# Four more channel tiles by block products, and the fifth product ahead of the seventh

## The chip, the cores and the metric

One core of one Trainium2 chip runs the whole block. The metric is the device time of one execution in microseconds: before, the median of three runs is 1000.0 us (999.8 to 1000.95). The engines are PE (TensorE), VectorE (DVE in the profile), ScalarE (ACT), GpSimd (POOL) and SyncE (SP), whose queue issues nearly all DMAs, one after the other.

## The reference

Everything is float32; x is 1 x 1024 x 1024, D_FF is 2816. The change is in the last product and the final norm, and in how the gated product before them is handed on.

```python
y = jnp.concatenate([y_a, y_b], axis=-1)             # short gated conv, conv module
x = x + jnp.einsum("bse,ed->bsd", y, w_out[l])
h = rmsnorm(x, norm_ffn_g[l])
g = dwconv(jnp.einsum("bsd,df->bsf", h, w_gate[l]), conv_ffn_w[l])
v = jnp.einsum("bsd,df->bsf", h, w_up[l])
x = x + jnp.einsum("bsf,fd->bsd", jax.nn.silu(g) * v, w_down[l])
return rmsnorm(x, norm_final_g)
```

## The kernel before

Channels lie on the 128 partitions, tokens along the row; the 1024 tokens are two halves of 512. D_FF is 22 channel tiles, the model width 8 tiles d (KD = 8). Each float32 product is three matmuls of 128x128 weights with 128x512 data, of rounded high parts and low remainders: hi by hi, hi by lo, lo by hi. Splitting costs a rounding on ACT (`whi`, `ahi`, or `r` for data) and a subtraction on DVE (`wlo`, `alo`, `r`).

**Block products.** Two products that share their data, or two neighbouring channel tiles by two token halves, are done as a 2x2 block product with seven instead of eight block products (class `Pair`, methods m1 to m7). Data operands are B11, B21, B22 and differences T1 to T4; weight operands are A11, A12, A22 and sums S1 to S4, which POOL forms (`s`) and ACT and DVE split. PSUM bank a takes m1, then m6, m7 and m4 on top; b takes m2; c takes m5 and then m3. After each product its method `after` reads the bank as it stands then and adds it into an output; the next product on that bank has to wait for that reading. In bank a, m7 therefore waits for the reading of m6, and m4 for that of m7.

**Gate and up** run f = 0 to 21, two tiles at a time. `ff_done` makes the tile t of the gated product (convolution by ACT and DVE, silu by ACT, product by DVE). For f up to 17 POOL makes four differences of a pair of tiles, and seven stores of 256 KB put the operands into the arrays yd in DRAM. The last four tiles are stored whole into `ytail`.

**Down** takes the 18 tiles in three chunks of six. In each chunk the eight d are four pairs (d, d+1) by six tiles, PPC = 3 block columns: a product is nine matmuls. Two pairs make a couple, so there are six couples (0 and 1 of chunk 0, 2 and 3 of chunk 1, 4 and 5 of chunk 2). In a couple, `STEPS` runs each product for both pairs: m1, then m3 of the couple before, m6, m2, m7, m5, m4. Couples 1 and 3 reload each operand for the next chunk right behind the product that used it last. The residual stream is read back from `x2d` into `xd0`, `xd2`, `xd3`, `xr0` and `xr1`; the last three take the room of the tiles t (`tp.release()`), so their loads wait for what reads those tiles. For couple 0 (`early`) ACT copies the bank a (`a1`) and POOL adds the copy; elsewhere DVE adds from the bank.

**The tail** multiplies the last four tiles plainly: for each of two halves and eight d, 4 tiles x 3 = 12 matmuls (`tail_mm`), 192 in all, the first half through before the second. The first half's final norm (sum of squares, a matmul with ones, root, reciprocal, products on POOL) lies beside the second half's matmuls. The second half's last output is done in three pieces of columns, with products on DVE (d < 5) and POOL.

PE follows the written order with few exceptions, and in the last part so do DVE, ACT and POOL. On the other queues the order comes from the scheduler, with work marked `urgent` first.

Of the kernel before, what the change touches and what calls it, by code (L numbers as in the profile page):

```python
# [13 lines left out]
P = 128  # L14
# [12 lines left out]
NTAIL = NF - 2 * NCH * PPC  # L27
# [18 lines left out]
def block_kernel(ctx: ExitStack, tc, xT, win01, win, wout, wgate, wup, wdown, consts, outT):  # L46
# [364 lines left out]
    yd = {o: dpool.tile([P, NCH * PPC, H], F32, name=f"yd{o}") for o in OPS}  # L411
    ytail = dpool.tile([NTAIL, P, S], F32, name="ytail")

# [90 lines left out]
    class Sums:  # L504
# [12 lines left out]
        def first(self, g, v):  # L517
# [4 lines left out]
            s1, s2 = self.both(hilo())  # L522
            return {"S1": s1, "S2": s2}
# [83 lines left out]
    def ff_done(f, g, v):  # L607
# [7 lines left out]
        if f >= NF - NTAIL:  # L615
            nc.sync.dma_start(ytail[f - (NF - NTAIL)], cc)
            return
# [110 lines left out]
    def ff_prep(f):  # L728
        raw, hl = g_job(f)
# [11 lines left out]
    with tc.manual_schedule(engines={nc.tensor.engine, V.engine}):  # L741
# [45 lines left out]
        p2.w.update(s2.second(g2[0], up2))  # L787
        plain[1].second_b()
# [5 lines left out]
    with tc.manual_schedule(engines={nc.tensor.engine}):  # L794
        for p in plain:
            p.finish()
        for f in range(NHEAD, NF - 2):
            p, q = fp[f], fp[f + 1]
            ff_prep(f + 1)
# [12 lines left out]

    W3 = PPC * P
    rblocks = [R[i][:, j, :] for i in (2, 3, 0, 1, 4, 5) for j in range(8)]

    def xblock(o, k, z):
        return rblocks[OPS.index(o) * 2 * PPC + z * PPC + k]
# [5 lines left out]
    def load_op(ch, o):  # L823
        for k in range(PPC):
            load_split(xblock(o, k, 0), xblock(o, k, 1), yd[o][:, ch * PPC + k, :])

    def load_d(p, tag, d, ch):
        t = p.tile([P, 2 * W3], F32, tag=tag, name=tag)
        f0 = 2 * PPC * ch
        for e in range(2):  # L830
            nc.sync.dma_start(
                t[:, e * W3 : e * W3 + W3].rearrange("p (f m) -> p f m", m=P),
                wdown[d, :, f0 : f0 + 2 * PPC].rearrange("p (f e) m -> p e f m", e=2)[:, e])
        return t

    w34 = [R[5][:, 2 + 3 * e : 5 + 3 * e, :].rearrange("p b t -> p (b t)") for e in range(2)]

    class Down(Pair):
        def __init__(self, ch, dp):
            super().__init__(PPC, lambda o, k: (xblock(o, k, 0), xblock(o, k, 1)))  # L840
            self.ch, self.dp, self.e = ch, dp, dp % 2
            self.early = ch == 0 and dp < 2

        def prep1(self):
            self.raw = load_d(wraw, "raw", 2 * self.dp, self.ch)
            hl = [t[:, : 2 * W3] for t in hilo()]
            split(self.raw, *hl, nc.vector)
            self.w.update(g_parts(hl, PPC))

        def prep2(self):  # L850
            self.up = load_d((rup, rup2)[self.e], "up", 2 * self.dp + 1, self.ch)
            self.s = Sums(PPC)
            self.w.update(self.s.first(self.raw, self.up))

        def prep3(self):
            t = w34[self.e]
            self.w.update(self.s.second(self.raw, self.up, a22p, (t[:, : 2 * W3], t[:, 2 * W3 :])))

# [39 lines left out]
    couples = [[Down(ch, 2 * i + e) for e in range(2)] for ch in range(NCH) for i in range(2)]  # L898

# [9 lines left out]
    STEPS = (("m6", "T2"), ("m2", "B21"), ("m7", "T3"), ("m5", "T1"), ("m4", "T4"))  # L909
# [37 lines left out]
    with tc.manual_schedule(engines={nc.tensor.engine}):  # L947
        for d in range(3, KD):
            load_xd(d)
        for i, pair in enumerate(couples):  # L950
            ch = pair[0].ch
            reload = i % 2 and ch + 1 < NCH
# [13 lines left out]
            for step, o in STEPS:  # L966
                for p in pair:
                    getattr(p, step)()
                if reload:
                    load_op(ch + 1, o)  # L970


    free = rblocks[:16]

    def yblock(h, i, z):
        return free[h * 8 + 2 * i + z]

    def load_tail(h):
        for i in range(NTAIL):
            load_split(yblock(h, i, 0), yblock(h, i, 1), ytail[i, :, h * H : h * H + H])  # L980

    tw = {}

    def tail_prep(dp):
        hl = hilo()
        for e in range(2):
            d = 2 * dp + e
            raw = wraw.tile([P, NTAIL * P], F32, tag="raw", name="rawt")
            nc.sync.dma_start(raw.rearrange("p (f m) -> p f m", m=P), wdown[d, :, NF - NTAIL :])
            a = e * NTAIL * P  # L990
            sl = [t[:, a : a + NTAIL * P] for t in hl]
            split(raw, *sl, nc.vector)
            tw[d] = parts(sl, 0, NTAIL)

    def tail_mm(b, d, h):
        for i in range(NTAIL):
            mm3(b, tw[d][0][:, i, :], tw[d][1][:, i, :], yblock(h, i, 0), yblock(h, i, 1), i == 0, i == NTAIL - 1)

    load_tail(0)
    tail_prep(0)  # L1000
    b0 = []
    with tc.manual_schedule(engines={nc.tensor.engine}):
        for d in range(2):
            b0.append(bank("y"))
            tail_mm(b0[d], d, 0)
        for p in couples[-1]:
            p.m3()
    load_tail(1)
    rf = rup.tile([P, S], F32, tag="up", name="rf")

    def scr(name):
        return cpy.tile([P, H], F32, tag="c", name=name)

    acc3 = wsum.tile([P, S], F32, tag="s", name="acc")
    accs = [half(acc3, h) for h in range(2)]
# [10 lines left out]
    def done(b, d, h):  # L1026
        x = half(xf[d], h)
        nc.vector.tensor_tensor(out=x, in0=b, in1=x, op=ALU.add)
        sq = scr("sq") if d else accs[h]
        nc.scalar.activation(sq, x, AF.Square)  # L1030
        if d and (h, d) != (1, KD - 2):
            nc.vector.tensor_tensor(out=accs[h], in0=accs[h], in1=sq, op=ALU.add)
# [14 lines left out]

    with tc.manual_schedule(engines={nc.tensor.engine}):
        for d in range(KD):
            if d >= 2:  # L1050
                if d % 2 == 0:
                    tail_prep(d // 2)
                b0.append(bank("y"))
                tail_mm(b0[d], d, 0)
            done(b0[d], d, 0)
            scale(d, 0)
    with tc.manual_schedule(engines={e.engine for e in (nc.tensor, nc.vector, nc.scalar, nc.gpsimd)}):
        for d in range(KD - 1):
            b = bank("y")
            tail_mm(b, d, 1)  # L1060
            if d == 1:
                m0 = total3(accs[0])
            s6 = done(b, d, 1)
            scale(d, 1)
            if d == 1:
                std = scr("std")
                nc.scalar.activation(std, m0, AF.Sqrt, bias=eps_r, scale=1.0 / D)
            if d == 2:
                nc.vector.reciprocal(rf[:, :H], std)
                for dd in range(KD):  # L1070
                    fin(dd, 0, 0, H, nc.gpsimd)
                    if dd % 2:
                        store(dd // 2, 0, 0, H)
        last = bank("y")
        tail_mm(last, KD - 1, 1)
        x = half(xf[KD - 1], 1)
# [10 lines left out]
        for (a, b), m in zip(PIECES, ms):  # L1087
            nc.scalar.activation(std[:, a:b], m[:, a:b], AF.Sqrt, bias=eps_r, scale=1.0 / D)
            if a == 0:
                scale(KD - 1, 1)  # L1090
# [7 lines left out]
    for p in (xlp, rup2, cpy, rup, wsum, xrp, a22p, psm, ps, dpool, wspl, wraw, apool, cpool):  # L1098
# [52 lines left out]
```

## Time and profile before

| | |
|---|---|
| median of three runs | 1000.0 us |
| profiled execution | 1000.93 us |
| its span | 999.1 us |
| instructions | 11602 |
| mean granted TensorE clock | 0.993 |
| matmul records on PE | 4208 |
| DMA, read and written | 84.79 and 27.00 MB |

Times in rows are microseconds from the span's start. A row of a timeline gives start, length, engine, line, operation, output and inputs, and how many instructions were drawn together; the bracket has the idle time before it and what ended it. Gate and up end near 760, couples 0 to 5 run from there to 933.8, the tail to 982, and what follows is the end of the norm. PE overlaps neighbouring matmuls, so the spacing of starts, not the length of one, tells its pace.

### The profile page before, as it was taken

What the parts mean: (1) busy time and instruction counts of PE and PEld (TensorE: products, weight loads), DVE (VectorE), ACT (ScalarE), POOL (GpSimd) and SP (SyncE); (2) the same over time, 40 slices, a digit from 0 to 9 for tenths busy, and PEclk for the clock granted to TensorE, in tenths of its full rate; (3) what the DMA queues carried; (4) which work ended last, traced back from release to release, by engine and by line L of the source; (5) the groups of instructions that cost most, each with busy time, mean ns of one, the idle gap of its engine ahead of it and who ended that gap; (6) DMA issues with size and microseconds to landing.
All of it is one profiled execution on the core that took longest, in us unless ns stands there. A gap on an engine that the chain in (4) does not pass through costs nothing.

```text
span 999.1 us, 11602 instructions
## 1 busy us (share of the span) xinstructions
PE 967.5 (97%) x4208; PEld 790.8 (79%) x4208; DVE 755.6 (76%) x888; ACT 452.8 (45%) x632; POOL 477.0 (48%) x303
## 2 busy tenths in 40 slices
PE   7999999999999999999999999999998999999994
PEld 5788888888878887788888888888886787878883
DVE  7899999999578897855655565565569798796556
ACT  7454422234564456434444443444457263544353
POOL 4289754353853006554455456365336744352006
PEclk9999999999999999999999999999999999999998
DMA  6211111113554204143143133134284663643105
GB/s 257 85 44 63 43 45 61 42 64 106 193 190 153 76 0 158 64 148 106 64 145 108 64 124 129 64 101 141 70 287 130 220 207 96 194 127 109 61 1 169
DMA packets 63274, 112.56 MB, mean 113 GB/s; under 512 B 5488, under 2 KB 27120, under 8 KB 62960
## 3 DMA queue, kind: packets, MB, share of 16 engines
q1 hardware_dynamic: 62640, 110.65, 33.1%
q10 hardware_dynamic: 576, 1.17, 0.3%
q8 instruction: 33, 0.54, 0.2%
q14 instruction: 25, 0.20, 0.1%
HBM read 84.79 MB, written 27.00 MB: 112 GB/s over the span
## 4 chain that ended last, share of the span: by engine, by line
PE 81%; DVE 9%; ACT 3%; issue 2%; DMA 1%; POOL 1%; POOLq 0%; SPq 0%; DVEq 0%; ACTq 0%
PE a L557 30%; PE mm L166 20%; PE c L557 15%; PE b L557 7%; DVE r L93 2%; PE c L692 1%; PE a L692 1%; PE mm L153 1%; PE mm L152 1%; PE mm L154 1%; PE y L154 1%; PE y L152 1%; PE y L153 1%; DMA raw<-wgate 1%; ACT whi L131 1%
## 5 line engine op out<-in xcount | busy, mean ns | idle before, releaser
L166 PE MATMUL mm<-r,whi 128*128 128x512 f32 x576 | 155.8, 389 | 0.0
L557 PE MATMUL a<-r,whi 128*128 128x512 f32 x472 | 145.7, 390 | 0.4 <-ACT a L542 0.4
L323 DVE SCALAR_TENSOR_TENSOR cv<-u,cst,cv 128x512 f32<-128x512 f32 x203 | 138.9, 751 | 1.7 <-ACT cv L317 1.2
L511 POOL TENSOR_TENSOR s<-raw,s 128x512 f32<-128x512 f32 (+1 forms) x31 | 57.5, 1854 | 161.5 <-DVE wlo L93 161.5
L166 PEld LDWEIGHTS mm<-r,whi 128*128 128x128 f32 x576 | 108.1, 188 | 22.6
L557 PE MATMUL c<-r,whi 128*128 128x512 f32 x392 | 121.1, 390 | 0.0
L93 POOL TENSOR_TENSOR wlo<-raw,whi 128x1024 fp32r<-128x1024 f32 x30 | 77.5, 2586 | 88.0 <-ACT whi L131 88.0
L131 ACT ACTIVATE whi<-raw 128x1024 fp32r<-128x1024 f32 (+1 forms) x68 | 69.2, 1020 | 103.5 <-PE mm L166 32.0
L557 PEld LDWEIGHTS a<-r,whi 128*128 128x128 f32 x472 | 88.4, 188 | 19.7 <-ACT a L542 0.8
L511 POOL TENSOR_TENSOR s<-up 128x512 f32<-128x512 f32 (+1 forms) x31 | 42.0, 1354 | 116.7 <-DMA up<-wup 96.8
L557 PE MATMUL a<-r,wlo 128*128 128x512 f32 x236 | 92.2, 391 | 2.8 <-DVE wlo L93 2.8
L166 PE MATMUL mm<-r,wlo 128*128 128x512 f32 x288 | 90.0, 389 | 0.0
L557 PEld LDWEIGHTS c<-r,whi 128*128 128x128 f32 x392 | 73.8, 188 | 16.0
L542 ACT ACTIVATE a<-a 128x512 f32<-128x512 f32 x80 | 47.5, 595 | 66.9 <-PE a L557 64.2
L131 ACT ACTIVATE whi<-s 128x1024 fp32r<-128x1024 f32 (+1 forms) x52 | 52.5, 1010 | 53.5 <-PE c L557 39.8
L557 PE MATMUL c<-r,wlo 128*128 128x512 f32 x196 | 76.5, 390 | 0.0
L635 DVE TENSOR_TENSOR t<-a,c 128x512 f32<-128x512 f32 x40 | 27.5, 687 | 64.4 <-ACT a L542 38.1
L557 PE MATMUL a<-r,ahi 128*128 128x512 f32 x224 | 70.5, 396 | 1.4 <-ACT a L542 1.4
L557 PE MATMUL b<-r,whi 128*128 128x512 f32 x232 | 71.4, 389 | 0.0
L93 DVE TENSOR_TENSOR wlo<-s,whi 128x1024 fp32r<-128x1024 f32 (+1 forms) x52 | 64.2, 1236 | 5.8 <-ACT whi L131 5.7
L131 ACT ACTIVATE r<-r 128x512 fp32r<-128x512 f32 x71 | 43.8, 628 | 49.8 <-DMA r<-ydB 23.3
L166 PEld LDWEIGHTS mm<-r,wlo 128*128 128x128 f32 x288 | 54.1, 188 | 11.2
(214 smaller groups left out, 2142.0 us busy)
## 6 DMA issues: line engine op xcount, KB each, us to landing
raw<-wgate SPq DMA_DIRECT2D x22, 512.0 KB, 4.9
up<-wup SPq DMA_DIRECT2D x20, 512.0 KB, 3.6
raw<-win SPq DMA_DIRECT2D x18, 512.0 KB, 3.2
ydT<-t SPq DMA_DIRECT2D x36, 256.0 KB, 3.4
r<-ydT SPq DMA_DIRECT2D x36, 256.0 KB, 3.3
raw<-wout SPq DMA_DIRECT2D x16, 512.0 KB, 3.4
ydB<-t SPq DMA_DIRECT2D x27, 256.0 KB, 5.0
r<-ydB SPq DMA_DIRECT2D x27, 256.0 KB, 4.5
```

The source lines that it names most:

```text
L93: eng.tensor_tensor(out=out, in0=a, in1=b, op=ALU.subtract)
L131: nc.scalar.activation(hi, y, AF.Copy)
L152: nc.tensor.matmul(out, whi, hi, start=first, stop=False)
L153: nc.tensor.matmul(out, whi, lo, start=False, stop=False)
L154: nc.tensor.matmul(out, wlo, hi, start=False, stop=last)
L166: nc.tensor.matmul(outs[h], w, a[h][z], start=s0, stop=s1)
L323: nc.vector.scalar_tensor_tensor(fin if k == KC - 1 else acc, src, w, acc, ALU.mult, ALU.add)
L511: self.eng.tensor_tensor(out=self.t[:, i * self.w : (i + 1) * self.w], in0=a, in1=b, op=op)
L542: nc.scalar.activation(t, b, AF.Copy)
L557: nc.tensor.matmul(out, w[wz][:, k, :], x[xz], start=first and k + wz + xz == 0, stop=k == n - 1 and wz == 1, skip_group_check=not first)
L635: nc.vector.tensor_tensor(out=out, in0=a, in1=b, op=op)
L692: nc.tensor.matmul(out, w[wz][:, k, :], xz, start=first and k == 0 and wz == 0 and xz is hi, stop=not first and k == 3 and wz == 1)
```

## The change

- `NTAIL` and `ytail` are gone. The last four channel tiles are a fourth chunk (`NPL` = 2 block columns, products of six matmuls) of four pairs `fin4` = a4, b4, c4, d4: 28 products, 168 matmuls. The tiles f = 18 to 21 thus get POOL's differences and seven stores per pair in place of one store of 512 KB per tile.
- For all four pairs the products that give the first token half (m1, m6, m2, m7, m4) come ahead of m5 and m3, which give the second.
- `STEPS` has m5 ahead of m7 in all couples, and T1 and T3 are both loaded behind m7. Couples 1, 3 and now 5 reload.
- Squares of the second half are partly added on POOL; in the three pieces DVE does 8, 6 and 5 of the eight products, not 5, 5 and 5.
- A gate weight load (`job`) is written ahead of `plain[1].second_b()`; no row of any engine stands elsewhere for it.

```diff
-NTAIL = NF - 2 * NCH * PPC
+NPL = NF // 2 - NCH * PPC
...
-        if f >= NF - NTAIL:
-            nc.sync.dma_start(ytail[f - (NF - NTAIL)], cc)
-            return
         ys[f] = cc
...
+    fin4 = [Down(NCH, dp) for dp in range(2)]
+    fin4 += [Down(NCH, 2 + e, rblocks[28 + 2 * e : 30 + 2 * e], rblocks[32 + 2 * e : 34 + 2 * e]) for e in range(2)]
+    couples.append(fin4[:2])
...
-    STEPS = (("m6", "T2"), ("m2", "B21"), ("m7", "T3"), ("m5", "T1"), ("m4", "T4"))
+    STEPS = (("m6", ("T2",)), ("m2", ("B21",)), ("m5", ()), ("m7", ("T3", "T1")), ("m4", ("T4",)))
...
-            reload = i % 2 and ch + 1 < NCH
+            reload = i % 2
...
+    def final(d, h, eng=nc.vector, first=0, alone=None):
         x = half(xf[d], h)
+        sq = scr("sq") if d != first else accs[h]
         nc.scalar.activation(sq, x, AF.Square)
+        if d not in (first, alone):
+            eng.tensor_tensor(out=accs[h], in0=accs[h], in1=sq, op=ALU.add)
+        scale(d, h)
         return sq
...
+        for p in (a4, b4):
+            p.m6()
...
+        for p in (a4, b4):
+            p.m2()
+            final(2 * p.dp, 0)
...
+        for p in (c4, d4):
+            p.m4()
+            final(2 * p.dp + 1, 0)
...
+        a4.m5()
+        b4.m5()
+        m0 = total3(accs[0])
+        final(1, 1, first=1)
+        std = scr("std")
+        nc.scalar.activation(std, m0, AF.Sqrt, bias=eps_r, scale=1.0 / D)
+        final(3, 1, nc.gpsimd, 1)
+        c4.m5()
+        nc.vector.reciprocal(rf[:, :H], std)
+        d4.m5()
+        final(5, 1, nc.gpsimd, 1)
+        final(7, 1, nc.gpsimd, 1)
+        for dd in range(KD):
+            fin(dd, 0, 0, H, nc.gpsimd)
...
+        a4.m3()
+        final(0, 1, first=1)
+        b4.m3()
+        final(2, 1, first=1)
+        c4.m3()
+        s6 = final(4, 1, first=1, alone=4)
+        d4.mul(d4.c, "S4", "B22", False)
...
-        for (a, b), m in zip(PIECES, ms):
+        for (a, b), m, n in zip(PIECES, ms, (KD, 6, 5)):
...
-                fin(d, 1, a, b, *((nc.vector, rp) if d < 5 else (nc.gpsimd,)))
+                fin(d, 1, a, b, *((nc.vector, rp) if d < n else (nc.gpsimd,)))
```

Three places show how instructions move. A row gives line, operation, output and inputs with the tile's size, and how many follow one another. Line numbers of the changed kernel are a few lower or higher.

The first is SP's queue of DMAs at the end of gate and up, while couple 0 runs. Before:

```order
L616 DMA ytail<-t 128x1024 x2
L907 DMA xd_5699<-x2d 128x1024
L907 DMA xr_5700<-x2d 128x1024 x2
L907 DMA xr_5701<-x2d 128x1024 x2
L831 DMA raw<-wdown 128x3x128 x2
```

And with the change, the names ydB and ydT standing for B11, T1, B21, B22 and then T2, T3, T4:

```order
L623 DMA ydB_1797<-t 128x512
L831 DMA raw<-wdown 128x3x128 x2
L623 DMA ydT_1792<-t 128x512
L831 DMA up<-wdown 128x3x128 x2
L623 DMA ydT_1794<-t 128x512
L831 DMA raw<-wdown 128x3x128 x2
L819 DMA r_96<-ydB_1791 128x512
L623 DMA ydT_1796<-t 128x512
L819 DMA r_96<-ydB_1791 128x512 x2
L831 DMA up<-wdown 128x3x128 x2
L912 DMA xd_5720<-x2d 128x1024
L912 DMA xr_5721<-x2d 128x1024 x2
```

The loads of xd3 (`xd_5699`, then `xd_5720`) and xr0 stood right behind the two stores; now the seven stores of the last pair, all loads of the next couple's weights and three of r stand ahead of them.

The second is ACT at the same time: `a_5840` and `a_5852` before, `a_5883` and `a_5895` after, are the copies of bank a behind m7 of couple 0; `whi<-s` rounds the sums S1, S2 of couple 1, and `t` is the last silu. Before:

```order
L131 ACTIVATE r_99<-s 128x768
L131 ACTIVATE whi<-raw 128x768 x2
L542 ACTIVATE a_5840<-a 128x512
L613 ACTIVATE t<-t 128x1024
L542 ACTIVATE a_5852<-a 128x512
L131 ACTIVATE whi<-s 128x768 x2
```

After:

```order
L131 ACTIVATE r_99<-s 128x768
L131 ACTIVATE whi<-raw 128x768 x2
L131 ACTIVATE whi<-s 128x768
L612 ACTIVATE t<-t 128x1024
L131 ACTIVATE whi<-s 128x768
L541 ACTIVATE a_5883<-a 128x512
L541 ACTIVATE a_5895<-a 128x512
```

Both copies are now behind both roundings of sums.

The third is DVE in couple 1, which is also how couple 3 reads; `xr` with input a is the reading of bank a, the first of each pair behind m7, that with c is behind m5. Before:

```order
L93 TENSOR_TENSOR r_94<-r_94,r_97 128x512
L863 TENSOR_TENSOR xr_5700<-xr_5700,a 128x512
L93 TENSOR_TENSOR r_94<-r_94,r_97 128x512
L863 TENSOR_TENSOR xr_5701<-xr_5701,a 128x512
L93 TENSOR_TENSOR r_94<-r_94 128x512 x2
L863 TENSOR_TENSOR xr_5700<-xr_5700,c 128x512
```

After:

```order
L93 TENSOR_TENSOR r_94<-r_94,r_97 128x512
L865 TENSOR_TENSOR xr_5721<-xr_5721,c 128x512
L93 TENSOR_TENSOR wlo<-s,whi 128x768
L93 TENSOR_TENSOR r_94<-r_94,r_97 128x512
L865 TENSOR_TENSOR xr_5722<-xr_5722,c 128x512
L93 TENSOR_TENSOR wlo<-s,whi 128x768
L93 TENSOR_TENSOR r_95<-r_95 128x512 x2
L865 TENSOR_TENSOR xr_5721<-xr_5721,a 128x512
```

The reading behind m7 now follows the two readings behind m5, two splits of sums, a split of B21 and two splits of T1 for the next chunk, and m4 of the first pair comes directly behind the second pair's m7 on PE.

More of the change, by code (lines that the diff above doesn't have):

```diff
@@ L949, in block_kernel @@
             load_xd(d)
-        for i, pair in enumerate(couples):
+        for i, pair in enumerate(couples[:-1]):
             ch = pair[0].ch
-            reload = i % 2 and ch + 1 < NCH
+            reload = i % 2
             for p in pair:
@@ L969, in block_kernel @@
                 if reload:
[L970 to L1009, printed above, removed]
+                    for o in ops:
+                        load_op(ch + 1, o)
+    tq = open_pool("tq", 1)
+    accs = [tq.tile([P, H], F32, name=f"acc3{h}") for h in range(2)]
+    rf = None
     def scr(name):
         return cpy.tile([P, H], F32, tag="c", name=name)
-    acc3 = wsum.tile([P, S], F32, tag="s", name="acc")
-    accs = [half(acc3, h) for h in range(2)]
     def total3(a):
@@ L1046, in store @@
         nc.sync.dma_start(outT[2 * dp : 2 * dp + 2, :, cols].rearrange("k p t -> p k t"), src)
+    a4, b4, c4, d4 = fin4
     with tc.manual_schedule(engines={nc.tensor.engine}):
[L1049 to L1056, printed above, removed]
-    with tc.manual_schedule(engines={e.engine for e in (nc.tensor, nc.vector, nc.scalar, nc.gpsimd)}):
[L1058 to L1076, printed above, removed]
```

94 lines of the change are left out of this document (62 added, 32 removed).

## The prediction

> **What bounds the kernel now.** I read the page's busy shares first, then the table of stretches, then the timelines of single engines where the changed code runs. In the table a row gives the stretch, its length, then busy time and count for PE, weight loads, DVE (VectorE), ACT (ScalarE) and POOL, then the granted clock, DMA share and GB/s.
>
> ```profile
> PE 967.5 (97%) x4208; PEld 790.8 (79%) x4208; DVE 755.6 (76%) x888; ACT 452.8 (45%) x632; POOL 477.0 (48%) x303
> ...
> 760.00:780.00 20.00, 15.50 (x58) 11.47 (x57) 20.00 (x15) 10.85 (x16) 19.02 (x11) 0.91 0.35 106
> ...
> 860.00:880.00 20.00, 20.00 (x89) 16.46 (x88) 20.00 (x27) 11.32 (x18) 9.62 (x7) 1.00 0.56 174
> 880.00:900.00 20.00, 19.56 (x87) 15.88 (x86) 17.76 (x23) 8.78 (x13) 8.37 (x6) 1.00 0.43 128
> ...
> 980.00:999.00 19.00, 5.76 (x29) 4.41 (x28) 12.84 (x26) 5.20 (x11) 10.61 (x14) 0.80 0.57 188
> ```
>
> PE sets the end: in the full stretch 860 to 880 it starts 89 matmuls, more closely one every 0.227 us (below: 796.08 - 787.89 = 8.19 for the 36 of four products). Nine (a product of three pairs) take 2.04 us and six 1.36. In the part that the change touches it loses time only at the seventh products of couples 0, 2 and 4 (rows below) and after 982. DVE is full or nearly so where this happens, and POOL with it in the first stretch. Whatever is put ahead of a DVE or POOL result there is paid by PE. Times below are those of the profiled execution (1000.93 us, span 999.1); the median is 0.9 less.
>
> **Couple 0: fifth ahead of seventh product.** Timeline rows: start, length, engine, line, output and inputs, and in brackets the idle time and its releaser.
>
> ```profile
> 769.98 0.61 PE L557 MATMUL a<-r,r 128*128 128x512 f32 x2
> 771.23 2.33 PE L557 MATMUL a<-r,r 128*128 128x512 f32 x9 [0.64 <-DVE r L93]
> ...
> 776.33 3.35 PE L557 MATMUL a<-r,r 128*128 128x512 f32 x7 [2.76 <-DVE r L93]
> 779.48 0.71 PE L557 MATMUL c<-r,whi 128*128 128x512 f32 x2
> ...
> 787.89 0.62 PE L557 MATMUL a<-r,whi 128*128 128x512 f32 x2
> ...
> 796.08 0.61 PE L557 MATMUL a<-r,whi 128*128 128x512 f32 x2
> ```
>
> Before, the two m7 wait 0.64 and 2.76 us for VectorE's splits of S3, and the seven matmuls behind the second wait take 3.15 us instead of 1.6: a clock loss of 1.5. With both m5 first (4.1 us from 769.98), m7 starts at 774.1 and ends at 778.2; both waits go. What is late next is m4(0). It adds to m7's bank, so it needs ACT's copy of m7, and in the order above that copy now stands behind two roundings of sums and a silu; the second sum comes from POOL.
>
> ```profile
> 774.26 2.01 DVE L93 TENSOR_TENSOR r<-s,r 128x768 fp32r<-128x768 f32 x1
> 781.52 2.32 DVE L614 TENSOR_TENSOR t<-t 128x1024 f32<-128x1024 f32 x1
> 789.37 0.69 DVE L863 TENSOR_TENSOR xd<-xd,a 128x512 f32<-128x512 f32 x1 [1.91 <-DMA xd<-x2d]
> ...
> 777.10 1.99 POOL L511 TENSOR_TENSOR s<-up 128x384 f32<-128x384 f32 x1
> 779.17 1.61 POOL L511 TENSOR_TENSOR s<-s,raw 128x384 f32<-128x384 f32 x1
> 788.30 1.01 POOL L511 TENSOR_TENSOR s<-raw,s 128x384 f32<-128x384 f32 x1
> 791.83 1.28 POOL L90 TENSOR_TENSOR xr<-xr,a 128x512 f32<-128x512 f32 x1
> ...
> 781.67 0.85 ACT L131 ACTIVATE whi<-s 128x768 fp32r<-128x768 f32 x1 [1.35 <-PE c L557]
> 790.16 0.60 ACT L542 ACTIVATE a<-a 128x512 f32<-128x512 f32 x1 [1.77 <-PE a L557]
> ...
> 774.36 9.84 SPq L616 DMA_DIRECT2D ytail<-t  x2
> 784.30 0.38 SPq L907 DMA_DIRECT2D xd<-x2d  x1
> 795.59 1.50 SPq L820 DMA_DIRECT2D r<-ydB  x3
> ...
> xr<-x2d SPq DMA_DIRECT2D x4, 512.0 KB, 6.3
> ytail<-t SPq DMA_DIRECT2D x1, 512.0 KB, 3.0
> ```
>
> POOL's first sum is done when its next operation starts, at 777.1; then a new difference t<-t (1.3 to 2.0, taken 1.7), 1.99, 1.61: 782.5. ACT: rounding 0.85, copy 0.60: 784.1. PE waits 5.9 us, and I charge the same clock loss of 1.5: m4 ends at 789.7 against 787.89. With POOL at its short rows (1.0 and 1.28) the copy comes at 781.9 and nothing is lost.
>
> Then m1 of couple 1 and m3(0) run to 795.8, and **m3(1) is late**. Its bank must first be read by VectorE into xd3, and xd3's load moved: before it was issued 0.1 us behind the second ytail store, now it stands behind seven stores for the tail pair, in one in-order queue. The last, ydT4, needs POOL's last difference. VectorE's product t, 2.32 long, moves behind two more instructions to 785.5 (the addition of c, 0.6, and a split, 0.95); POOL then does an addition, two t, two s and the last t: six operations of 1.01 to 1.6, about 1.3 each, from 785.9 to 793.8. Behind ydT4 the queue issues two loads of r (0.5 each) and two of up, and xd3 goes out at 796.3. Before, VectorE used it 5.1 us after issue (784.30 to 789.37), waiting on it; with 4.7 it is there at 801. Addition 0.7, m3(1) 2.04, a second clock loss 1.5: couple 1's m6 starts at 805.3, not 796.08. **Term: +9.2.** Bounds: POOL at its short rows and a load of 3.0 (the DMA view's landing of the ytail store) give +4.7; POOL at 1.6 and a load of 6.3 (that of the four xr loads) give +12.4.
>
> On the clock loss, the Trainium skill (TensorE: Matmul & The Clock Gate, What's actually happening) puts the drop to half speed behind an idle window of about 3.4 us, and as long again of work to undo it; the wait of 2.76 above already shows it. By its figures the two long waits lose some 1.7 each, an estimate, and the term would be +9.6.
>
> **Couples 1 and 3.** Here T1 and T3 are both loaded behind m7, and m4(0) needs VectorE's addition of m7.
>
> ```profile
> 810.89 0.67 DVE L863 TENSOR_TENSOR xr<-xr,a 128x512 f32<-128x512 f32 x1
> 813.89 0.68 DVE L863 TENSOR_TENSOR xr<-xr,c 128x512 f32<-128x512 f32 x1
> 814.49 0.95 DVE L93 TENSOR_TENSOR wlo<-s,whi 128x768 fp32r<-128x768 f32 x1
> 815.36 0.68 DVE L93 TENSOR_TENSOR r<-r 128x512 fp32r<-128x512 f32 x1
> 817.66 2.93 DVE L93 TENSOR_TENSOR r<-r 128x512 fp32r<-128x512 f32 x2
> 868.97 0.68 DVE L863 TENSOR_TENSOR xr<-xr,a 128x512 f32<-128x512 f32 x1
> ...
> 812.40 0.63 PE L557 MATMUL a<-r,ahi 128*128 128x512 f32 x2
> 871.49 0.63 PE L557 MATMUL a<-r,ahi 128*128 128x512 f32 x2
> 834.52 3.67 PE L557 MATMUL a<-r,r 128*128 128x512 f32 x15 [1.41 <-DVE xd L863]
> 892.64 3.66 PE L557 MATMUL a<-r,r 128*128 128x512 f32 x15 [0.44 <-DVE xd L863]
> ```
>
> Seven instructions newly stand ahead of that addition: two of c and three of r at 0.6 (813.89 to 814.49), two wlo<-s at 0.87: 4.8 us. In an engine as full as before the addition ends at 810.89 + 4.8 + 0.6 = 816.3, and m4(0), due at 812.40, waits 3.9; in couple 3, 868.97 + 5.4 = 874.4 against 871.49: 2.9. If PE's long waits let VectorE catch up, the wait falls towards nothing, but POOL's sums of this couple run beside it (two splits took 2.93 there, not 1.36). Between 0 and 3.9, and 0 and 2.9, I take 2.6 and 2.0, two thirds, as the row with POOL beside it is the nearer one. The waits of couples 2 and 4 (1.41, 0.44) go, since m5's 4.1 us cover them. **Term: +4.6 - 1.8 = +2.8**, bounds -1.8 and +5.0. Couple 5 also reloads, but ten matmuls of the next chunk and of m3 lie between m7 and m4: nothing, as long as VectorE is within 2.3 us.
>
> The Trainium skill (SBUF — State Buffer, Who interferes with whom) has VectorE and POOL exclude each other for a whole instruction when VectorE reads two SBUF operands. The pair at 2.93 agrees, while additions from PSUM keep 0.68; by it a split could wait out a POOL operation of up to 2.0, and the term would reach its upper bound.
>
> **The tail.** 192 plain matmuls become 168: 24 x 0.227 = -5.4 for PE. But the last matmul isn't the end.
>
> ```profile
> 970.91 3.35 DVE L1069 RECIPROCAL rf<-std 128x512 f32<-128x512 f32 x1
> 977.55 1.66 DVE L1032 TENSOR_TENSOR acc<-acc,sq 128x512 f32<-128x512 f32 x1 [0.70 <-ACT sq L1030]
> 982.68 0.34 DVE L1080 TENSOR_TENSOR xr<-y,xr 128x192 f32<-128x192 f32 x1
> ...
> 974.40 5.95 POOL L1037 TENSOR_TENSOR xd<-xd,rf 128x512 f32<-128x512 f32 x4 [63.03 <-DVE rf L1069]
> ...
> 987.79 1.15 DVE L1037 TENSOR_TENSOR xd<-xd,rp 128x192 f32<-128x192 f32 x4 [0.40 <-ACT rf L1093]
> ```
>
> Before, matmuls of the second half lay beside the norm of the first. Now the first half's last m4 ends at 933.80 (start of the tail) + 150 x 0.227 = 967.8, nothing covers its sum, and 36 matmuls follow (8.2 us). From 967.8 one chain leads to the first piece: addition 0.6, square 0.65, sum 0.7, matmul 0.9, root 0.7, wait for an addition 0.9, reciprocal 3.35, addition 0.6, square 0.65, POOL's new sum 1.3, sum 0.7, addition 0.6, square 0.65, sum beside POOL's products 1.65, addition 0.6: 14.6, with some 0.05 per hand-over 15.3. First piece at 983.1, against 982.68. PE itself is done at 979. So the 5.4 are eaten by VectorE, and four more products at 0.29 (1.15/4) in the pieces add 1.2. **Term: +1.6**, bounds -4.2 (all 5.4 kept) and +3.
>
> **At nothing:** `job` moves no instruction. The pair 18/19 gets four POOL operations and 0.75 MB more of stores in 735 to 757; PE's matmuls there are ten us and more from the loads behind them, without which cover it is 0.7.
>
> **Sum:** +9.2 + 2.8 + 1.6 = +13.6: 1014.5 against 1000.93, 1013.6 against the median.
>
> **Rivals.** (1) Couple 0 costs only its lower bound and VectorE has caught up by couple 3: +4.7 + 0.5 + 1.6 = +6.8, 1006.8. For it: POOL's rows of 1.0 at 788; against: VectorE is 100% busy until 785, and POOL's rows beside that are 1.6 to 2.2. (2) **Not slower:** VectorE and POOL hardly meet, because PE's waits spread their work. Every split then takes 0.69, every POOL sum 1.0, the product t 1.2: xd3 goes out at 793.3, lands in 3.0, m6 starts at 799.1 (+3.0); couples 1 and 3 don't wait (-1.8); the tail follows PE (-3.2 + 1.2 = -2.0): -0.8, 999.2. It decides if POOL's rows behind 777 have a mean under 1.1. Against it: the rows at 777 and 779. (3) The upper bounds of couples 0 and 1 meet: +12.4 + 5.0 + 1.6 = +19, 1019.
>
> **How the numbers follow.** Forecast (1008 to 1018) 0.57, rival 1 (1001 to 1008) 0.2, rival 2 (under 1001) 0.15, rival 3 0.08. A measurement tells 0.2% from no change: under 998 is 0.1 (half of rival 2 and what beats it), within 998 to 1002 is 0.07, above is 0.83. The range runs from 1000 to 1018.5, leaving out 0.11 below and 0.08 above.
>
> **What would show it.** Right: no wait at m7 of couples 0, 2, 4; at m4(0) of couple 0 a wait of 4 to 6 us for ACT's copy; at m3(1) one of 4 to 7 for VectorE, which waits for the load of xd3, issued after 794; 1 to 4 us at m4 of couples 1 and 3; some 2 us at the total in the tail; the first piece 3 us or more behind the last product. Wrong, if xd3 is issued before 789 or VectorE's first piece follows the last matmul at once.

## The result, and the profile after

The changed kernel is slower, by two and a half times what was forecast: 1033.22 us median (1030.51 to 1035.42) against 999.9 us, a ratio of 1.0331 with an interval of 1.030 to 1.0361. The profiled execution took 1035.42 us, its span is 1033.3 us against 999.1, so the trace has 34.2 us to explain. One execution of the kernel with both copies, below, took 1590.72 us at a granted clock of 0.571 and is left out of its median.

Here are the first part of the page after, and rows of its table of stretches with the same columns as before. The stretch 1000 to 1033 answers to 980 to 999 of before.

```profile
PE 976.4 (95%) x4184; PEld 796.6 (77%) x4184; DVE 771.0 (75%) x911; ACT 461.6 (45%) x650; POOL 507.4 (49%) x330
...
780.00:800.00 20.00, 12.11 (x45) 9.53 (x45) 11.27 (x10) 5.06 (x8) 15.41 (x11) 0.83 0.49 158
...
860.00:880.00 20.00, 20.00 (x89) 16.46 (x88) 10.32 (x15) 6.32 (x11) 8.73 (x8) 1.00 0.51 152
880.00:900.00 20.00, 16.20 (x62) 12.84 (x61) 17.28 (x25) 10.35 (x17) 5.87 (x4) 0.83 0.55 164
...
960.00:980.00 20.00, 16.82 (x62) 13.05 (x61) 16.59 (x24) 9.31 (x18) 8.70 (x10) 0.83 0.11 31
...
1000.00:1033.00 33.00, 16.53 (x56) 12.96 (x56) 21.31 (x37) 12.64 (x22) 17.29 (x16) 0.72 0.38 127
```

The count behind PE is what to read: 89 matmuls fill 20 us, and three of these stretches start only 45 to 62. In each of those three the granted clock is below 1 as well, so PE loses twice, by waiting and by running slowly afterwards. The stretch 860 to 880 is as full as before: where PE doesn't wait, its pace is the same.

The view of waits names what PE waits for between 735 and 1030. A row gives the waiting engine, its output and line, whom it waits for, then the sum, the times and the longest, in us.

```profile
PE c L556 <- DVE xd L865: 8.7, 1, 8.7
PE a L556 <- DVE xr L865: 7.4, 2, 3.8
PE a L556 <- ACT a L541: 6.8, 3, 5.8
PE total L1086 <- DVE acc L1000: 4.6, 1, 4.6
PE a L556 <- DVE xd L865: 2.3, 1, 2.3
PE total L988 <- DVE acc L1000: 2.2, 1, 2.2
```

All but the totals are waits for a PSUM bank that has not been read yet: c at m3(1) in couple 1, a at m4 of couples 1 and 3 (7.4 in two), a at m4(0) of couple 0 (5.8 of the 6.8), and a once more in the tail. The number in brackets is the pair: m4(0) is m4 of a couple's first pair, and m3(1) is m3 of couple 0's second pair, which runs within couple 1.

The last row of products in the timeline of PE, and the first of the pieces in VectorE's:

```profile
1000.76 10.32 PE L556 MATMUL c<-r,r 128*128 128x512 f32 x36
```

```profile
1016.11 0.34 DVE L1083 TENSOR_TENSOR xr<-c,xr 128x192 f32<-128x192 f32 x1
```

PE is done with them at 1011.1, 5.0 us ahead of the first piece, where before the first piece followed at once.

Starts of the same product in both timelines of PE cut the 34.2 us into the prediction's terms:

| from, to | before | after | grown by | predicted |
|---|---|---|---|---|
| start, behind m2 of couple 0 | 769.98 | 771.57 | 1.6 | 0 |
| to m6 of couple 1 | 796.08 | 810.11 | 12.4 | 9.2 |
| to m6 of couple 5 | 913.28 | 936.65 | 9.3 | 2.8 |
| to the end of the last product | 982.5 | 1011.1 | 5.2 | -3.2 |
| to the end of the span | 999.1 | 1033.3 | 5.6 | 4.8 |

### The profile page after: what moved, and what is told of

Its sections match the earlier page's. It is cut to its first block, busy times and chain, and to the rows that moved or that the text cites. A ratio compares the mean times of both kernels' runs of the same rounds, so it can differ in the third digit from the quotient of the medians.

```text
span 1033.3 us, 11698 instructions
## 1 busy us (share of the span) xinstructions
PE 976.4 (95%) x4184; PEld 796.6 (77%) x4184; DVE 771.0 (75%) x911; ACT 461.6 (45%) x650; POOL 507.4 (49%) x330
## 3 DMA queue, kind: packets, MB, share of 16 engines
q1 hardware_dynamic: 68144, 113.79, 33.3%
## 4 chain that ended last, share of the span: by engine, by line
PE 73%; DVE 10%; issue 5%; DMA 5%; POOL 3%; ACT 3%; SPq 0%; POOLq 0%; DVEq 0%; ACTq 0%
PE a L556 28%; PE mm L166 19%; PE c L556 13%; PE b L556 6%; DVE r L93 3%; POOL s L510 2%; PE c L688 1%; PE a L688 1%; DMA xd<-x2d 1%; PE mm L154 1%; PE mm L153 1%; PE mm L152 1%; DVE wlo L93 1%; DMA c<-xT 1%; DMA raw<-wgate 1%
## 5 line engine op out<-in xcount | busy, mean ns | idle before, releaser
L556 PE MATMUL a<-r,whi 128*128 128x512 f32 x496 | 155.5, 395 | 0.2 <-ACT a L541 0.2
L510 POOL TENSOR_TENSOR s<-raw,s 128x512 f32<-128x512 f32 (+2 forms) x35 | 61.8, 1767 | 162.3 <-DVE wlo L93 153.8
L131 ACT ACTIVATE whi<-raw 128x1024 fp32r<-128x1024 f32 (+2 forms) x72 | 71.7, 998 | 108.5 <-PE b L556 36.9
L556 PEld LDWEIGHTS a<-r,whi 128*128 128x128 f32 x496 | 94.5, 191 | 21.0 <-ACT a L541 0.6
L510 POOL TENSOR_TENSOR s<-up 128x512 f32<-128x512 f32 (+2 forms) x35 | 45.8, 1310 | 119.5 <-DMA up<-wup 97.6
L556 PE MATMUL a<-r,wlo 128*128 128x512 f32 x248 | 97.9, 395 | 2.9 <-DVE wlo L93 2.9
L556 PE MATMUL a<-r,ahi 128*128 128x512 f32 x240 | 80.1, 416 | 14.5 <-DVE xr L865 7.4
L90 POOL TENSOR_TENSOR t<-t 128x512 f32<-128x512 f32 x44 | 67.7, 1550 | 20.1 <-DVE t L613 20.1
L131 ACT ACTIVATE whi<-s 128x1024 fp32r<-128x1024 f32 (+2 forms) x54 | 53.8, 996 | 47.4 <-PE c L556 33.9
L93 DVE TENSOR_TENSOR wlo<-s,whi 128x1024 fp32r<-128x1024 f32 (+2 forms) x54 | 66.6, 1234 | 5.8 <-ACT whi L131 5.7
```

What stands on the lines that cost most here:

```text
L90: nc.gpsimd.tensor_tensor(out=out, in0=a, in1=b, op=op)
L93: eng.tensor_tensor(out=out, in0=a, in1=b, op=ALU.subtract)
L131: nc.scalar.activation(hi, y, AF.Copy)
L510: self.eng.tensor_tensor(out=self.t[:, i * self.w : (i + 1) * self.w], in0=a, in1=b, op=op)
L556: nc.tensor.matmul(out, w[wz][:, k, :], x[xz], start=first and k + wz + xz == 0, stop=k == n - 1 and wz == 1, skip_group_check=not first)
```

## The experiments

The theory after the result: the new order moves the reading of the bank that frees PE behind other work in an in-order queue, on VectorE in couples 1 and 3, on ScalarE in couple 0, and on SP (the load of xd3) ahead of m3(1). The rivals: the engines have too much work wherever the banks are read, or the four channel tiles cost the time whatever the order. Each ratio is against the kernel before on the same chip.

| kernel | median us | before | ratio, 95% interval |
|---|---|---|---|
| after | 1033.22 | 999.9 | 1.0331 (1.030 to 1.0361) |
| after, old order of products | 1010.17 | 1000.36 | 1.0096 (1.0081 to 1.0111) |
| before, new order of products | 1016.35 | 1000.36 | 1.0154 (1.0139 to 1.017) |
| that, bank a copied in couples 1, 3 | 1005.57 | 1000.25 | 1.0062 (1.0046 to 1.0078) |
| after, bank c copied in couple 0 | 1028.01 | 1000.36 | 1.0275 (1.0259 to 1.029) |
| after, both copies | 1019.49 | 1000.49 | 1.0193 (1.0173 to 1.0213) |
| before, with the added stores | 1006.66 | 1000.49 | 1.0059 (1.0044 to 1.0074) |
| after, other weight tiles in the tail | 1029.89 | 1000.36 | 1.0291 (1.0274 to 1.0308) |
| after, reciprocal earlier | 1029.97 | 1000.25 | 1.0304 (1.029 to 1.0318) |
| after, old order, all mends together | 1009.96 | 1000.25 | 1.0096 (1.0081 to 1.011) |
| before, new order in couples 2, 4 | 999.74 | 1000.25 | 0.9996 (0.9987 to 1.0005) |
| that, bank a copied there | 998.44 | 1000.57 | 0.9982 (0.9973 to 0.9991) |

### The two halves of the change apart

After, with the old order of products:

```diff
-    STEPS = (("m6", ("T2",)), ("m2", ("B21",)), ("m5", ()), ("m7", ("T3", "T1")), ("m4", ("T4",)))
+    STEPS = (("m6", ("T2",)), ("m2", ("B21",)), ("m7", ("T3",)), ("m5", ("T1",)), ("m4", ("T4",)))
```

> The changed kernel with the old order of products (seventh ahead of fifth, T3 loaded behind the seventh and T1 behind the fifth); the fourth chunk by products stays. Theory (the order of the products makes the waits at m4): the waits at m4 of couples 0, 1 and 3 with the slow clock behind them (about 7.8, 5.6 and 6.6 us) go, the old ones at m7 of couples 0, 2 and 4 come back (about 7 in all), the wait of m3 for xd3's load stays at some 8 us: about 1020 us. Rival (the added work of the fourth chunk loads VectorE and POOL, and the order of products matters little): within 4 us of 1033.

Before, with the new order, is the same line the other way round.

> The kernel before with the new order of products alone (fifth ahead of seventh, T1 and T3 both loaded behind the seventh); the last four tiles stay plain. Theory: m4 waits some 4 us in couple 0 and 4 each in couples 1 and 3, with 1.5 to 2.5 of slow clock behind each, the old waits at m7 (about 7 us) go, xd3's load is in time: +8 to +11, about 1010 us. Rival (the order is harmless without the stores): within 2 us of 1000.

The order is worth 23 us in the kernel after (1033.2 to 1010.2), and 16 us alone. The four tiles alone cost 9.8 us; 16.0 and 9.8 leave 7.5 of the 33.3 us to the two together. Both theories named the right side and missed the size: the old order gains 10 us more than expected, the new order alone costs 5 to 8 us more. Waits of PE from 760 on with the old order after:

```profile
PE a L556 <- DVE r L93: 3.4, 2, 2.8
PE c L556 <- DVE xd L865: 3.3, 1, 3.3
```

The waits at m7 are those of before (3.4 in two). That for xd at m3(1) is 3.3, and was expected to stay near 8: the four tiles bring it, and the new order makes it 8.7. With the new order alone, couples 1 and 3 are worse than in the kernel after, not better; the timelines of PE and then of VectorE in couple 1 of that kernel:

```profile
807.87 4.24 PE L557 MATMUL a<-r,r 128*128 128x512 f32 x18
820.64 1.22 PE L557 MATMUL a<-r,ahi 128*128 128x512 f32 x2 [8.53 <-DVE xr L863]
```

```profile
803.84 1.41 DVE L93 TENSOR_TENSOR r<-r 128x512 fp32r<-128x512 f32 x2 [4.56 <-ACT r L131]
...
813.37 0.68 DVE L863 TENSOR_TENSOR xr<-xr,c 128x512 f32<-128x512 f32 x1
813.97 0.94 DVE L93 TENSOR_TENSOR wlo<-s,whi 128x768 fp32r<-128x768 f32 x1
814.84 0.68 DVE L93 TENSOR_TENSOR r<-r,r 128x512 fp32r<-128x512 f32 x1
815.44 0.68 DVE L863 TENSOR_TENSOR xr<-xr,c 128x512 f32<-128x512 f32 x1
816.04 1.15 DVE L93 TENSOR_TENSOR wlo<-s,whi 128x768 fp32r<-128x768 f32 x1
817.11 2.88 DVE L93 TENSOR_TENSOR r<-r 128x512 fp32r<-128x512 f32 x2
819.91 0.67 DVE L863 TENSOR_TENSOR xr<-xr,a 128x512 f32<-128x512 f32 x1
```

PE is done with both m7 at 812.1 (807.87 + 4.24), and the first pair's bank a is read at 819.91. From 803.84 on VectorE works without a gap, in the end at the seven instructions that the prediction had counted. It starts late, since its reload splits had waited 4.56 us for ScalarE's roundings, and ScalarE 6.65 us for the reload's DMA. The first row is ScalarE's, the second VectorE's split at the same place in the kernel before, 2.5 us earlier:

```profile
803.18 1.35 ACT L131 ACTIVATE r<-r 128x512 fp32r<-128x512 f32 x2 [6.65 <-DMA r<-ydB]
```

```profile
801.30 2.52 DVE L93 TENSOR_TENSOR r<-r 128x512 fp32r<-128x512 f32 x2 [2.29 <-ACT r L131]
```

And the seven take 6.5 us (813.37 to 819.91), not 4.8: the two splits at 817.11 take 2.88 beside GpSimd's sums, where the prediction had counted 0.6 for each.

So 8.5 us are lost in couple 1 (and 2.7 more to the clock), where the bound of the prediction was 3.9.

### Is it the queue or the work?

The same kernel, with bank a behind m7 copied out by ScalarE in couples 1 and 3 and added by GpSimd, as couple 0 does:

```diff
-            if self.early:
+            if self.early or (m, self.ch < 2, self.dp >= 2) == (1, True, True):
                 self.add_copy(m, h, copy_of(self.a, "a1"))
```

> The kernel before with the new order of products alone (as the run of that alone, 1016.4 us), where in couples 1 and 3 ACT copies bank a behind m7 and POOL adds the copy, so that m4 needn't wait for VectorE's queue. Theory (m4 waits because the reading stands behind some 16 us of work in VectorE's in-order queue): the waits of 8.7 and 4.3 us at m4 fall to 0 to 3 each, and the slow clock behind them goes too: 1002 to 1007 us. Rival (m4 waits for the loads of T1, whoever reads the bank, since ACT's copies also stand behind their rounding): 1012 us or longer.

Four readings leave VectorE, and 10.8 of the 16.0 us come back (1016.35 to 1005.57). The wait in couple 1 falls to 0.9 and that in couple 3 to 0.3; 2.8 us of waiting turn up at m4 of couple 2 instead. What cost the time was mostly the queue in which the reading stood, and not how much there was to do: the four readings themselves are 2.7 us of VectorE's work, at 0.68 each.

### m3(1), and why mends don't add up

After, with bank c of couple 0 copied by ScalarE, so that m3(1) no longer waits for xd3:

```diff
-            self.add(1, 1, self.c)
+            if self.early:
+                self.add_copy(1, 1, copy_of(self.c, "c1"))
+            else:
+                self.add(1, 1, self.c)
```

> The changed kernel, where in couple 0 ACT copies bank c behind m5 and POOL adds the copy (as is done there for bank a), so that m3 doesn't wait for xd3's load. Theory: the wait of 8.9 us at m3 of couple 0 goes, with 1.6 of slow clock: -8 to -10.5, about 1023 to 1025 us, with m4 of couple 1 waiting as before. Rival (the engines are behind there anyway, and the next product waits instead): less than 4 us are won.

Its waits for a bank between 760 and 1030:

```profile
PE a L556 <- DVE xr L865: 14.9, 2, 10.8
PE a L556 <- ACT a L541: 5.8, 1, 5.8
```

The wait of 8.7 is gone, but only 5 us come back, of the 8 to 10.5 expected: at m4 of couple 1 the wait rose from 3.6 to 10.8. While PE stood at m3(1), VectorE had caught up. The wait at m3(1) had hidden most of the wait behind it, which is why couple 1 looked milder in the kernel after than with the order alone. Then both copies at once, the last two diffs on the kernel after:

> The kernel after, with bank c of couple 0 and bank a behind m7 of couples 1 and 3 copied out by ScalarE, so that VectorE's queue stands ahead of no bank that m3(1) or m4 of couples 1 and 3 waits for. Theory (the order of the products costs what it does because PE waits for VectorE's in-order queue, and each copy alone only uncovered the next wait): with all of them gone at once the couples lose their waits, m3(1) under 2 us, m4 of couples 1 and 3 under 1 us each, with the clock losses behind them; 1012 to 1016 us. Rival (the work of VectorE and ScalarE is what PE runs into, wherever the banks are read): the waits move on to m7 of the even couples or to the weights' tiles; 1022 us or longer.

It lies between the two: 13.7 us come back, of the 17 to 21 of the theory. m3(1) no longer waits, and m4 of couple 3 waits 0.1 us; m4 of couple 2 now waits 1.9. In couple 1 the reading has changed engines and is late again. PE and ScalarE there:

```profile
814.68 1.29 PE L556 MATMUL a<-r,r 128*128 128x512 f32 x5
820.53 1.22 PE L556 MATMUL a<-r,ahi 128*128 128x512 f32 x2 [4.55 <-ACT a L541]
```

```profile
813.45 1.96 ACT L131 ACTIVATE r<-r 128x512 fp32r<-128x512 f32 x3 [4.97 <-DMA r<-ydT]
...
818.34 1.66 ACT L131 ACTIVATE r<-r 128x512 fp32r<-128x512 f32 x3
819.90 1.06 ACT L541 ACTIVATE a<-a 128x512 f32<-128x512 f32 x2
```

ScalarE had 5 us of nothing to do, waiting for a reload's DMA, and then ran eleven roundings of operands and sums ahead of the copy. The queue explains it here too; my theory had the wait gone because the copy was on another engine, and that step was wrong.

### What the stores alone cost

Before, with the differences and seven stores per pair for the last four tiles added (what they store is not used):

```diff
-    yd = {o: dpool.tile([P, NCH * PPC, H], F32, name=f"yd{o}") for o in OPS}
+    yd = {o: dpool.tile([P, NF // 2, H], F32, name=f"yd{o}") for o in OPS}
...
             nc.sync.dma_start(ytail[f - (NF - NTAIL)], cc)
-            return
```

> The kernel before, with GpSimd's differences and the seven stores of the first half's rows for the last four channel tiles added beside the stores of the old tail; what they store is not used, and the tail is the old one. Theory (about a third of what the four tiles cost comes ahead of the tail, from these stores: 0.6 us at the end of the feed-forward part and the wait of m3(1) for the late xd3): a wait of 2 to 4 us at the first product that reads xd3 in couple 1, and about 1004 us. Rival (the stores cost nothing there, all that the four tiles cost comes from the tail): no such wait, within 1 us of the kernel before.

It costs 6.2 us, more than expected, with no change of order and with the old tail. SP's queue, and PE at m3(1):

```profile
783.45 1.24 SPq L626 DMA_DIRECT2D ydB<-t  x2
785.93 3.85 SPq L626 DMA_DIRECT2D ydT<-t  x3
791.72 0.38 SPq L830 DMA_DIRECT2D raw<-wdown  x1
792.19 0.44 SPq L906 DMA_DIRECT2D xd<-x2d  x1
```

```profile
798.48 2.08 PE L557 MATMUL c<-r,r 128*128 128x512 f32 x4 [6.92 <-DVE xd L862]
```

The load of xd3 goes out at 792.19, not 784.30, behind the stores. This kernel stores the last four tiles twice, into `ytail` and into yd, and makes GpSimd's differences as well, so it does more than the change and doesn't tell stores from differences. In the changed kernel with the old order, m3(1) waits 3.3 us, not 6.9. There m6 of couple 5 is 5.1 us late (918.4 for 913.3) and the end 9.1 us, so of what the four tiles cost by themselves the tail has 4.0.

### The tail

Three kernels mend parts of it. After, with the second weights of the last two pairs loaded into the free half of their first tile, because the load of `up` had to wait in SP's queue, 7.4 us long, for VectorE's last reading of the old tile:

```diff
-            self.up = load_d((rup, rup2)[self.e], "up", 2 * self.dp + 1, self.ch)
+            self.up = load_d((rup, rup2)[self.e], "up", 2 * self.dp + 1, self.ch, self.t_up)
```

> The changed kernel, where the last two pairs' second weight tiles are loaded into the free halves of their first tiles, not into the buffers that the pairs ahead still use, so that their sums can be made some 8 us earlier. Theory (the wait of a4's m7 is VectorE standing at the split of c4's sums, whose load came late): the waits of 2.4 and 1.1 us there and the slow clock behind them go: -4 to -6.5, about 1027 to 1029 us. Rival (VectorE is simply full there): within 2 us of 1033.

At the m7 of the tail's first two pairs, the kernel after waits 2.29 and 0.89 us, and the 14 matmuls from 974.42 take 5.96 us for 3.18:

```profile
971.89 1.64 PE L556 MATMUL a<-r,r 128*128 128x512 f32 x6 [2.29 <-DVE xd L865]
974.42 2.90 PE L556 MATMUL a<-r,r 128*128 128x512 f32 x6 [0.89 <-ACT whi L131]
...
980.38 0.62 PE L556 MATMUL c<-r,whi 128*128 128x512 f32 x2
```

With the other tiles the waits there are 1.4 and 0.4 us with no loss of clock, and the kernel is 3.3 us shorter by the medians (the two intervals just overlap), where 4 to 6.5 were expected. After, with VectorE's reciprocal right behind the root:

```diff
+        nc.vector.reciprocal(rf[:, :H], std)
         final(3, 1, nc.gpsimd, 1)
         c4.m5()
-        nc.vector.reciprocal(rf[:, :H], std)
```

> The changed kernel with VectorE's reciprocal of the first half's norm ahead of its readings of the fifth products, not between them. Theory (the end is VectorE's chain, not the last matmul): the reciprocal starts some 2 us earlier, at the root's end, and the wait of 4.7 us ahead of the last totals gets shorter by 1.5 to 2: -1.5 to -2, about 1031. Rival (the last products on PE or POOL's products set the end): within 0.7 of 1033.

From the first total to the end it is 31.7 us instead of 33.1. The rest of the 3.2 us by which its median is shorter lies ahead of that, in waits and clock, and the intervals overlap; PE still waits ahead of the last totals, since VectorE now waits for GpSimd's sum. Third, after with the old order of products, the copy of c, the other weight tiles, and the total ahead of all eight products m5 and m3, with the reciprocal behind it:

> The changed kernel with the old order of products (1010.2 us alone), bank c copied in couple 0, the second weight tiles in their own room, and at the end the total of the first half ahead of the fifth products of the first two pairs, so that 48 matmuls, not 36, lie beside the norm, with the reciprocal right behind the root. Theory: the wait of 3.5 us at m3 of couple 0 goes, and the waits ahead of the last totals fall from 4.3 to about 1: 1002 to 1004 us. Rival (the end is VectorE's and POOL's work, whatever lies beside it): only the 3.5 are won, 1006.5 us or longer.

It gains nothing on the old order alone (1009.96, 1010.17), where 6 to 8 us were expected. The 3.3 us at m3(1) are gone, but m4 of couple 1 now waits 1.5 us and m7 of couple 2 3.2, not 1.1. Its total waits as before, and so do the last totals, although 48 matmuls lie between:

```profile
972.24 1.13 PE L994 MATMUL total<-acc,ones_r 128*128 128x512 f32 x2 [2.18 <-DVE acc L1006]
...
988.84 1.01 PE L1092 MATMUL total<-acc,ones_r 128*128 128x192 f32 x2 [4.57 <-DVE acc L1006]
```

In these runs the end follows the chain of additions, squares and sums on VectorE, GpSimd and ScalarE, and the matmuls moved did not shorten it. But the reciprocal isn't right behind the root here: two readings of m5 stand ahead of it in VectorE's queue.

```profile
976.75 3.35 DVE L1066 RECIPROCAL rf<-std 128x512 f32<-128x512 f32 x1
```

It starts 4.5 us behind the total (972.24), as in the kernel after (4.75), and not 2.0 us behind it as in the run with the reciprocal moved alone (997.88 for 995.88). What the two together would bring is not shown.

### A place where the new order pays

Before, with m5 ahead of m7 in couples 2 and 4 only, where nothing is reloaded:

```diff
+    EVEN = tuple(STEPS[k] for k in (0, 1, 3, 2, 4))
...
-            for step, o in STEPS:
+            for step, o in EVEN if i in (2, 4) else STEPS:
```

> The kernel before, with the fifth product ahead of the seventh in couples 2 and 4 alone, which reload nothing. Theory (the order loses only where VectorE has new data to split ahead of the reading): the old waits there, 1.6 and 0.6 us, go and no new one comes: -1.5 to -2.2, about 998 us. Rival (m4 then waits in the same way): 0 or longer.

The waits at m7 are gone, as the prediction had it, but m4 of couple 2 waits 1.2 us for its bank: no difference, as the rival had it. With that bank copied out by ScalarE in these couples,

```diff
-            if self.early:
+            if self.early or (m, self.ch > 0, self.dp < 2) == (1, True, True):
```

> The kernel before, with m5 ahead of m7 in couples 2 and 4 only, and there the bank a behind m6 and m7 copied out by ScalarE and added by GpSimd. Theory (the new order pays only where the bank that is freed last stands in a queue that is not behind): the waits of 1.4 and 0.4 us at m7 are gone and the 1.33 us that the same order without the copy had at m4 of couple 2 go as well; 998.0 to 998.8 us, a gain of 0.1 to 0.2%. Rival (ScalarE's copy stands behind its roundings there too, as in couple 1 of the run with both copies): a wait of 1 us or more at m4 of couple 2 or 4, 1000 to 1002 us.

no wait is left in them (the edit copies bank a behind m7 alone, the copy that m4 needs, and not behind m6), and the kernel is 2.1 us faster than before (0.9982, interval 0.9973 to 0.9991): the shortest of all these kernels.

## Why the prediction was wrong

**The direction was right, and so was the mechanism in the couples; their sizes were not, and in the tail a wait was missing.** Forecast +13.6, range up to 1018.5; measured 1033.2. Of the 20.6 us that the trace has beyond the sum (34.2 for 13.6), 1.6 lie ahead of couple 0, 3.2 in couple 0, 6.5 in couples 1 to 4 and 9.2 in the tail.

**Couple 0, +9.2, measured +12.4: right in its mechanism.** Both m7 run without a wait. m4(0) waits for ScalarE's copy, as said, 5.8 us where 5.9 was predicted; m1 of couple 1 then starts at 791.52, and 789.7 with the late start of 1.6 makes 791.3. ScalarE's rows show the copy behind the two roundings and the silu:

```profile
778.79 0.85 ACT L131 ACTIVATE whi<-s 128x768 fp32r<-128x768 f32 x1 [4.41 <-POOL s L510]
779.93 1.06 ACT L612 ACTIVATE t<-t 128x1024 f32<-128x1024 f32 x1 [0.29 <-DVE t L611]
784.35 0.84 ACT L131 ACTIVATE whi<-s 128x768 fp32r<-128x768 f32 x1 [3.35 <-POOL s L510]
785.10 1.07 ACT L541 ACTIVATE a<-a 128x512 f32<-128x512 f32 x2
```

What was mis-sized is the wait for xd3: 8.75 us for 5.9. The queue and the reader:

```profile
796.68 0.38 SPq L623 DMA_DIRECT2D ydT<-t  x1
...
798.13 1.10 SPq L831 DMA_DIRECT2D up<-wdown  x2
799.27 0.53 SPq L912 DMA_DIRECT2D xd<-x2d  x1
```

```profile
803.32 2.08 DVE L93 TENSOR_TENSOR r<-r 128x512 fp32r<-128x512 f32 x2
805.84 0.69 DVE L865 TENSOR_TENSOR xd<-xd,c 128x512 f32<-128x512 f32 x1 [0.43 <-DMA xd<-x2d]
```

It went out at 799.27, not 796.3 (1.6 of that from the late start), and took 6.6 us to the reader, not 4.7, which was less than the 5.1 of its own rows (784.30 to 789.37); the upper bound, 6.3, was the right end. The load isn't alone in it: two splits of reloaded data stand ahead of the reading in VectorE's queue and ended at 805.4, so an earlier landing by itself would have won no more than the 0.43 us for which VectorE stood idle.

**Couples 1 to 4, +2.8, bounds -1.8 and +5.0, measured +9.3: a step that failed.** The waits of couples 2 and 4 went, as predicted. Those at m4 of couples 1 and 3 are 3.60 and 3.80 us, where 2.6 and 2.0 were taken and 3.9 and 2.9 were the bounds, and the clock behind them, charged at nothing, lost 1.6 and 2.4 (m4 takes 830.20 to 835.95 and 893.13 to 899.75, against 4.20 before). The bounds were wrong too: they let VectorE start its seven instructions no later than before, and priced the splits at 0.6 although the prediction itself shows a pair at 2.93. The run with the order alone shows 8.5 in couple 1. Of the 4.6 us beyond the bound of 3.9, 2.5 are the late start, from the reload's chain of DMA, ScalarE and VectorE, and 1.7 the slower instructions.

**The tail, +1.6, measured +10.8: the step that failed by most.** The wait at the total, forecast at 2.2, is 2.18. The end follows VectorE's chain: the first piece comes 5.0 us behind the last product, forecast 4.1, and the pieces grew by 0.8, forecast 1.2. The chain from the last m4 of the first half took 18.1 us (998.0 to 1016.11) against 15.3; 1.4 of it is the place of the reciprocal. What failed is PE's side, which I had put at 24 matmuls saved and the rest at full pace. From m6 of couple 5 to the end of the last m4 of the first half it took 61.4 us (936.65 to 998.0), forecast 54.5 (913.28 to 967.8): this 6.8 and the 2.8 of the chain make up the tail's miss, less 0.4 in the pieces. In it are the two waits at m7 of the first two pairs and the clock behind them, 3.2 and 2.7, which the sum had at nothing. Behind it PE lost 2.2 more at the total, 1.3 of clock and a gap of 1.0 that the view lays to nothing, but there the end follows VectorE. I had looked at the tail's norm and not at its weights. The prediction's opening, too, reads VectorE as full or nearly so behind 982, where its row has 12.84 of 19 us.

**The end of gate and up, at nothing, measured +1.6:** three waits, of 0.8, 0.2 and 1.1 us, against 0.4 and 0.7 before; the remainder was not traced. The term had 0.7 as its price without cover.

**The clock, charged twice at 1.5.** The kernel after loses some 11 us to it in six places up to the last product, against 1.6 in one place before. Every wait of 2 us or more should have had a loss of 0 to 3 us of its own in the range.

**The rivals.** The one on the other side fell at its own condition: GpSimd's twelve operations behind 777 have a mean of 1.56 us (from 1.73 at 777.03 to 1.29 at 795.09), not under 1.1.

The third, with both upper bounds, pointed the right way and still was 14 us short.

## What to carry to other kernels

When a product is moved ahead, look for the reader of the bank that the next product needs and price what then stands ahead of it on its in-order engine, starting from when that queue itself can start, and not from when it started before. A wait that is seen may hide the next one: before a term is set at what one profile shows, ask what the engine behind it does in the meantime; one mend here took away a wait of 8.7 us and gained 5. And stores are paid in the queue, by the load that stands behind them, even where the DMA engines are busy for half of the time (0.49 in 780 to 800).

## What was not expected of the hardware

A wait of the same length costs the clock a different amount. The second m7 of couple 0, first in the kernel after with the old order, then in that with the added stores:

```profile
776.99 2.14 PE L556 MATMUL a<-r,r 128*128 128x512 f32 x7 [2.76 <-DVE r L93]
778.93 1.06 PE L556 MATMUL c<-r,whi 128*128 128x512 f32 x2
```

```profile
775.25 1.88 PE L557 MATMUL a<-r,r 128*128 128x512 f32 x7 [2.62 <-DVE r L93]
```

Before, the same seven matmuls behind the same 2.76 us took 3.35. Summing what the starts behind a wait are apart beyond 0.227 us, the loss was some 1.6 us there. With the old order it was 1.7, mostly in the products behind m7, where pairs take 1.06 us; with the added stores it was nothing.

The record of the granted clock in the traces shows what makes the difference. The half-speed stretches are whole blocks of 3.41 us, and in a trace they all start on one grid of such blocks, whenever the waits came: in the kernel after at 782.22, 802.70, 830.00, 891.44, 973.36 and 1000.67, which are 6, 8, 18, 24 and 8 blocks apart. In all thirteen traces, from 735 to the last totals, a block at full speed in which PE, by the profile's times, stood idle for 1.9 us or more was followed by one at half speed, and one with 1.8 us or less was not. Before, 2.66 of the 2.76 us lay in the block that ends at 776.23, and the clock dropped there; with the added stores a block ends at 774.07, in the middle of the wait, with 1.44 us of it on one side and 1.18 on the other. With the old order the block ends at 778.48, behind the wait, and so the loss comes later.

What is lost is half of what is left of the half-speed blocks once PE works again. The 8.75 us at m3(1) cost only 1.5: the blocks from 802.70 end at 809.53, and PE starts again at 806.58. With the order alone, 3.9 us at m4(0) cost 1.7, 4.1 us in couple 3 cost 2.96 and 8.5 us in couple 1 cost 2.74.

The Trainium skill (TensorE: Matmul & The Clock Gate, What's actually happening) has the clock set by how busy PE has been in a window of 3413 ns that runs freely. The grid in these traces agrees. The 1.7 us that the prediction worked out from that window as the loss per wait is not a bound: up to 2.96 was measured. It may be why the kernel after spreads over 5 us between executions and the one before over 1.5; that was not tested.
